# Scores of two heads together, biases read ready-made, a split last output column, and a planner with other durations

## The chip, the cores and the metric

The kernel runs as one launch on one core of a Trainium2 chip. The metric is device microseconds (us) of that core, all shapes and types as the reference gives them (float32 throughout). A core has a tensor engine (PE, with weight loads shown apart as PEld), a vector engine (DVE), a scalar engine (ACT), a GpSimd engine (POOL), a sync engine (SP) that here issues all large DMAs, an SBUF, and a PSUM of eight banks of 128 x 512 float32 into which PE writes.

## The reference, cut to what matters

Two transformer blocks over 256 tokens and a model width of 2048, batch 1, one layer each.

```
# block 1: native sparse attention + conformer conv, then a conv-GLU FFN (5632 wide)
h = rms_norm(x); proj = h @ w_in                       # q, kv of 3 branches, gates, conv input
for each of 16 heads (4 kv heads): three softmaxes
    compressed: 15 block keys   s = q.k_cmp + bias[bucket(t - (16 n + 31))], masked
    selected, window: 256 keys  s = q.k     + bias[bucket(t - s)], masked (causal)
    out = gate_0 * p_cmp v_cmp + gate_1 * p_sel v_slc + gate_2 * p_win v_win
u = a * sigmoid(gate); depthwise conv of 31 taps; layer_norm; silu
x += concat(attention, conv) @ w_out
x += conv_glu_ffn(rms_norm(x));  x = rms_norm(x)
# block 2: MLA + gated linear attention, then a gated FFN, both modulated by ada = silu(c) @ w_ada
x += gate_m * rms_norm(mix(h) @ w_out)
f  = (silu(h @ w_gate) * (h @ w_up)) @ w_down          # 5632 wide
x += gate_f * rms_norm(f)
```

With 256 tokens there are four selection blocks and all of them are chosen, so the selected and the window branch are plain causal attention over 256 keys of 64 channels.

## The kernel before

**Weights and the main stream.** All weight matrices lie in DRAM in the order in which they are used, cut into chunks of 128 x 1024 (`MCS`). `load_raw` brings chunks from SP's queue. For precision each chunk is split in two float32r parts, `wh` on ACT (`split_h`) and `wl` on DVE (`split_l`), three chunks ahead (`LA`); `wh` has four buffers and `wl` three. Activations lie split in the same way (high and low part). A product is then three float32r matmuls: high x high, high x low, low x high (`run_group`). A chunk of two K tiles and four output tiles takes 24 matmuls of 256 columns. Groups (`GROUPS`) run in a fixed order: w_in (conv input c0, c1, kvc, c2, kk, gt, q0, q1, c3, vv, q2, q3), w_out in three parts (oa: heads' outputs 0 to 3, ob: 4 to 7, oz: the conv's channels), FFN 1, block 2 and last `g2_0` to `g2_3`, the down projection: its weights (512 columns) move, the tokens are stationary, and the two halves of 128 tokens (u = 0, 1) have a bank each. A group owns two or four of the eight PSUM banks until its evacuation.

**The planner.** While the program is written out, Python keeps an estimated clock per engine (`Clock.note`: cost by columns). All work that is not the main stream is a generator ("side"). `tick`, called every two K tiles, issues a step of a side if its inputs are ready by the estimated PE clock; a low-priority side (the conv) only runs while the estimated DVE clock is at most `LAG` = 1 us ahead of PE's. `need(n)` holds a step until n banks are free and, unless over 3 us of the group are left, enough stay over for the next group. `later` postpones an evacuation until PE's estimated end. The engines run what they were given in that order; a wrong estimate shows as a wait on the chip. Nearly every instruction is issued by one helper, line 306, so the rows say L306 and the tile names tell them apart.

**Side work of block 1.** `conv_gen`: 31 taps on 8 channel tiles on DVE (tile `cacc`), then the layer norm, whose result `ch`, `cl` is the input of the oz groups. `bias_gen`: a one-hot table (`oht`) times the 32 x 16 bias table on PE, once for distances (then stored to DRAM as `dtab` and read back per head pair, skewed, as tile `B`) and in 15 matmuls of 16 columns for the compressed keys (`cbias`). `att_gen`, per head: scores against `kz` (keys of one kv head in 64 of 128 rows, the other 64 rows zero, so that a 128-row q tile of two heads can be used) and `kcz`, 512 + 256 + 2 x 16 columns in float32, which PE does in two passes each; on DVE bias, mask and maximum (one custom instruction per branch, an add and a maximum for the compressed keys); exp and scaling on ACT; eight transposes on PE; copies `PT` on ACT; then per pair the products with V. `att_driver` starts a head when the one before has its scores and when the head `PB` = 3 before it is transposed.

**The end.** `finish` follows the last matmul: for each token half sum of squares, root, reciprocal, four multiply-adds of 512 columns on DVE and their four stores.

Of the kernel before, what the change touches and what calls it, by code (L numbers as in the profile page):

```python
# [143 lines left out]
PB = 3  # L144
# [4 lines left out]
AHEAD = 2  # L149
SKIP = 48  # L150
# [43 lines left out]
OH = Layout([("ohr", 384), ("ohf", 512)])  # L194
CA = Layout([("mix_g", 16), ("ffn_g", 16), ("relb", 16), ("cmask", 32), ("conv_w", 248), ("conv_b", 8), ("ln_g", 8),
# [3 lines left out]
OFF_C = 271  # L199
# [14 lines left out]
def _onehot(dist, width):  # L214
    o = np.zeros((128, width), np.float32)
    i = np.arange(len(dist))
    o[_bucket(dist), i] = 1.0
    o[32, i] = dist < 0
    return o


def pack_small(inp):
# [21 lines left out]
    for tt in range(2):  # L244
        cm[:, tt, :15] = (16 * np.arange(15)[None] + 31) <= (tt * 128 + t)[:, None]
    relb = np.zeros((33, 16), np.float32)
    relb[:32] = f["rel_bias"][:, HORD]
    relb[32] = NEG
    pos = f["cmp_pos"][0]
    oh = put(OH, dict(ohr=_onehot(np.arange(384) - 127, 384), ohf=_onehot(np.arange(512) - OFF_C, 512)))  # L250
    ca = put(CA, dict(
        mix_g=cols(f["mix_norm_g"][0]), ffn_g=cols(f["ffn_norm_g"][0]), relb=relb,
        cmask=cm.reshape(128, 32), conv_w=f["conv_w"][0].reshape(31, 8, 128).transpose(2, 1, 0).reshape(128, 248),
# [27 lines left out]
    return dict(vec=vec, fv=fv, oh=oh, ca=ca, cb=cb, w1=c(w1), wada=c(wada), x=c(x), pos=c(f["positions_2"]))  # L281
# [12 lines left out]

class Engine:
# [5 lines left out]
    def __getattr__(self, op):  # L301
        f = getattr(self.eng, op)

        def issue(*x, **k):
            self.clock.note(self.name, op, x)
            return f(*x, **k)  # L306
        return issue


class Clock:  # L310
# [4 lines left out]
    def __init__(self):  # L315
        self.t = dict(PE=0.0, DVE=0.0, ACT=0.0)
        self.dep, self.ends, self.n, self.last = 0.0, {}, 0, None

    def note(self, eng, op, x):
# [18 lines left out]
        start = max([self.t[eng], self.dep] + [v + self.LAT for k, v in self.ends.items() if k != eng])  # L338
# [35 lines left out]
class Kern:  # L374
    def __init__(self, nc, tc, a, dump=None, stop=None):
# [11 lines left out]
        self.hl = {}  # L387
# [140 lines left out]
    def later(self, f, norm):  # L528

        self.pending.append((self.clock.t["PE"] + Clock.LAT, f, norm))  # L530
# [21 lines left out]
    def run_group(self, g):  # L552
# [5 lines left out]
        src = self.src  # L558
# [10 lines left out]
        kl = len(g["ks"]) - 1  # L569
# [3 lines left out]
        for mi in g["mcs"]:  # L573
# [6 lines left out]
            h, l = self.next_mc(mi)  # L580
            t["PE"] = max(t["PE"], self.l_end.pop(mi))
            for u in range(nt if g["mode"] == "w" else 2):
                o = ps[u][:min(n, 128)] if g["mode"] == "w" else ps[u][:, :n]
                for q, k in enumerate(m["ks"]):
                    xh, xl = src(k, N)
                    if g["mode"] == "w":
                        c = slice(q * n + u * 128, q * n + u * 128 + min(n, 128))
                        p = ((h[:, c], xh), (h[:, c], xl), (l[:, c], xh))
                    else:
                        c, ts = slice(q * n, q * n + n), slice(u * 128, u * 128 + 128)  # L590
                        p = ((xh[:, ts], h[:, c]), (xl[:, ts], h[:, c]), (xh[:, ts], l[:, c]))
                    for i, (a, b) in enumerate(p):
                        self.mm(o[:, :b.shape[1]], a, b, k == 0 and i == 0, k == kl and i == 2)
                    if q % GRAN == GRAN - 1 and (u, k) != (nb - 1, m["ks"][-1]):
                        self.tick()
            self.emitted += 1
            if mi != g["mcs"][-1]:
                self.tick()
        ev = self.evac[key]
# [5 lines left out]
        self.tick()  # L605

# [127 lines left out]
    def build(self):  # L734
        nc, tc = self.nc, self.tc
        with ExitStack() as es:
# [10 lines left out]
            with ExitStack() as ph:  # L747
# [12 lines left out]
                if not self.stop:  # L760
                    self.finish()
# [26 lines left out]
    def block1_setup(self):  # L788
# [12 lines left out]
        self.kz = P.tile([128, 4, 2, T], F32, name="kz")  # L801
        self.V = P.tile([128, 2, 2, 4, 64], F32, name="V")
        self.Gt = P.tile([128, 2, 8, 2, 3], F32, name="Gt")
        self.cbias = P.tile([128, 2, 8, 2, 16], F32, name="cbias")
        self.kcz = P.tile([128, 4, 16], F32, name="kcz")
# [6 lines left out]
        g.memset(self.kz, 0.0)  # L812
        g.memset(self.kcz, 0.0)
        g.memset(self.vz, 0.0)
        g.memset(self.cbias, NEG)
# [26 lines left out]
        self.side(self.bias_gen())  # L842
# [105 lines left out]
    def bias_gen(self):  # L948
        while "ss" not in self.flags:
            yield  # L950
        oh = self.early.tile([128, OH.n], F32, name="oht", tag="g2")
        self.sy.dma_start(oh, self.a["oh"])
        ohr, ohf = (oh[:33, o:o + n] for o, n in OH.at.values())
        yield 8.0
        yield from self.need(1)
        o = self.bank()
        self.mm(o[:16, :384], self.ca("relb", 0, 16)[:33], ohr)
        yield
        tr = self.early.tile([16, 384], F32, name="tabr", tag="tok")
        self.act(tr, o[:16, :384], AF.Copy)  # L960
        self.free(o)
        self.dtab = self.dp.tile([16, 384], F32, name="dtab")
        self.sy.dma_start(self.dtab, tr)
        yield
        yield from self.need(1)
        bk = self.bank()
        o = bk[:, :256].rearrange("p (n h) -> p n h", n=16)
        for w in range(15):
            c = OFF_C - 31 + 128 - 16 * w
            self.mm(o[:, w], ohf[:, c:c + 128], self.ca("relb", 0, 16)[:33])  # L970
        yield

        for tt, w, n in ((0, 8, 7), (1, 0, 15)):
            self.v.tensor_copy(self.cbias[:, tt].rearrange("p a u n -> p (a u) n")[:, :, :n],
                               o[:, w:w + n].rearrange("p n h -> p h n"))
        self.free(bk)

# [8 lines left out]
    def cmp_gen(self):  # L986
        yield
        for kv in range(2):
# [23 lines left out]
            if kv == 0:  # L1012
# [3 lines left out]
                dst = self.kcz.rearrange("p (b u) n -> p u b n", u=2)  # L1016
                for u in range(2):
                    pr = slice(64 * u, 64 * u + 64)
                    self.v.tensor_copy(dst[pr, u, :, 0:15], src[pr, u])
# [75 lines left out]
    def att_driver(self):  # L1095
# [10 lines left out]
        for n in range(16):  # L1106
            while f"q{n // 2}" not in self.flags or n >= PB and f"T{n - PB}" not in self.flags or \
                    n and f"S{n - 1}" not in self.flags:
                yield
            self.side(self.att_gen(n))  # L1110
            yield ATT
# [5 lines left out]
    def load_B(self, p):  # L1117
        B = self.att.tile([128, 2, T], F32, name="B", bufs=2)
        d = self.dtab
# [4 lines left out]
    def att_gen(self, n):  # L1124
# [3 lines left out]
        h = 2 * (p // 4) + u  # L1128
        q = self.qT[p]
        yield  # L1130
        yield from self.need(2)
        S1, S0 = self.bank(), self.bank()
        self.mm(S1, q[:, 128:], self.kz[:, h].rearrange("p r s -> p (r s)"))
        self.mm(S0[:, 0:256].rearrange("p (r s) -> p r s", r=2), q[:, :128], self.kz[:, h, :, :128])
        for tt in range(2):
            self.mm(S0[:, 256 + 16 * tt:272 + 16 * tt], q[:, tt * 128:tt * 128 + 128], self.kcz[:, h])
        self.flags.add(f"S{n}")
        yield
# [6 lines left out]
        rs = A.tile([128, 2, 3], F32, name="rs", bufs=6)  # L1145
        for r in range(2):
# [6 lines left out]
        self.free(S1, S0)  # L1153
        if u == 0 and p < 7:
# [6 lines left out]
        for tt in range(2):  # L1161
            self.act(sc[:, tt], sc[:, tt], AF.Exp, bias=mx[:, tt, 0:1], accum_out=sm[:, tt, 0:1])
# [6 lines left out]
        for tt in range(2):  # L1169
            self.stt(Pc[:, tt, 0:16], sc[:, tt], rs[:, tt, 0:1], self.ca("cmask", 16 * tt, 16), OP.mult, OP.mult)  # L1170
# [780 lines left out]
    def tok_gen(self):  # L1951
# [6 lines left out]
        self.ssq = self.f2.tile([128, 2, 4], F32, name="ssq")  # L1958
# [41 lines left out]
    def finish(self):  # L2000
        R = self.rp.tile([128, T], F32, name="sd")[:, :2]
        x = self.XT.rearrange("p (c a) t -> p c (a t)", a=2)
        for tt in range(2):
            r, f = R[:, tt:tt + 1], self.f[:, tt, 1536:]
            self.square(f, tt, 3)
            self.v.tensor_reduce(r, self.ssq[:, tt], axis=AX, op=OP.add)
            self.act(r, r, AF.Sqrt, scale=1.0 / D, bias=self.eps)
            self.tt(f, f, self.gpb[1][:, 1], OP.mult)
            self.v.reciprocal(r, r)
            for j in range(4):  # L2010
# [25 lines left out]
```

## Time and profile before

| | |
|---|---|
| median of 3 runs | 2206.18 us (2204.81 to 2206.24) |
| profiled execution | 2205.54 us, span 2203.8 us from the first to the last instruction |
| PE, PEld | 98%, 94% of the span busy, 17465 matmuls |
| DVE | 77% |
| ACT | 53% (1179.5 us) |
| POOL | under 1% |
| DMA | 496.51 MB from SP's hardware queue, 63.6% of 16 engines' span |
| chain that ended last | PE 89%, DVE 6%, ACT 2%, issue 1%, DMA 1% |

The page's busy share of PE is an upper bound, since matmuls are pipelined and their ends modelled; starts are what is measured. In the tables of stretches a row is: stretch, length, then for PE, PEld, DVE, ACT and POOL the busy us and the number of instructions, then the granted share of PE's clock, the DMA engines' share and GB/s.

### The profile page before, as it was taken

The numbers are of one execution on the slowest core, as the hardware profiler recorded it, in microseconds if no ns is written. First come the engines' busy times: TensorE is split into PE (matmuls) and PEld (weight loads), VectorE is DVE, ScalarE is ACT, GpSimd is POOL, SyncE is SP. The second block draws the span as 40 slices with busy tenths as digits, with TensorE's granted clock in tenths as the row PEclk, the third lists the DMA queues.
The fourth block names the chain that finished last, engine by engine and source line by source line (L and its number), as shares of the span: only waits on it lengthen the run. The fifth ranks groups of instructions, "written<-read, shape, count | busy, mean of one in ns | idle before, by whom it ended". The sixth has DMA issues, their size and how long they took to land.

```text
span 2203.8 us, 42192 instructions
## 1 busy us (share of the span) xinstructions
PE 2167.6 (98%) x17465; PEld 2081.5 (94%) x17465; DVE 1692.8 (77%) x2611; ACT 1179.5 (54%) x1805; POOL 5.1 (0%) x18
## 2 busy tenths in 40 slices
PE   8999999999999999999999999999999999999997
PEld 7998889999999999999999889989998999899986
DVE  7998988999998699999988666678676665554455
ACT  5447686655553355555556664466444444444443
POOL 0000000000000000000000000000000000000000
PEclk9999999999999999999999999999999999999999
DMA  6554325788888788888855334646776775555553
GB/s 232 192 178 152 130 82 194 254 322 325 310 326 323 276 316 316 323 319 306 302 201 180 134 134 137 209 153 211 251 260 244 254 252 189 194 188 176 192 194 131
DMA packets 86784, 499.20 MB, mean 227 GB/s; under 512 B 9648, under 2 KB 12096, under 8 KB 40128
## 3 DMA queue, kind: packets, MB, share of 16 engines
q1 hardware_dynamic: 86592, 496.51, 63.6%
q8 instruction: 136, 2.23, 0.4%
q14 instruction: 56, 0.46, 0.1%
HBM read 494.35 MB, written 2.12 MB: 225 GB/s over the span
## 4 chain that ended last, share of the span: by engine, by line
PE 89%; DVE 6%; ACT 2%; issue 1%; DMA 1%; SPq 0%; DVEq 0%; ACTq 0%
PE ps L306 89%; DVE wl L306 2%; DMA raw<-in_wst_dram 1%; DVE cacc L306 1%; ACT wh L306 0%; DVE X L306 0%; DVE ac L306 0%; ACT L306 0%; DVE og L306 0%; ACT P L306 0%; DVE nt L306 0%; ACT X L306 0%; ACT ge L306 0%; DVE XT L306 0%; DVE ss L306 0%
## 5 line engine op out<-in xcount | busy, mean ns | idle before, releaser
L306 PE MATMUL ps<-X,wh 128*128 128x256 f32 (+1 forms) x7680 | 1330.3, 277 | 5.1 <-ACT X L306 2.9
L306 ACT ACTIVATE wh<-raw 128x1024 fp32r<-128x1024 f32 (+2 forms) x741 | 782.8, 1058 | 837.6 <-PE ps L306 781.2
L306 DVE TENSOR_TENSOR wl<-raw,wh 128x1024 fp32r<-128x1024 f32 (+2 forms) x741 | 898.9, 1215 | 393.8 <-PE ps L306 339.4
L306 PEld LDWEIGHTS ps<-X,wh 128*128 128x128 f32 x7680 | 1161.5, 188 | 11.4 <-ACT X L306 3.5
L306 PE MATMUL ps<-X,wl 128*128 128x256 f32 (+1 forms) x3840 | 1060.2, 276 | 4.8 <-DVE wl L306 4.8
L306 PEld LDWEIGHTS ps<-X,wl 128*128 128x128 f32 x3840 | 722.1, 188 | 6.0 <-DVE wl L306 6.0
L306 DVE SCALAR_TENSOR_TENSOR ac<-wa,cs,ac 128x512 f32<-128x512 f32 x360 | 269.5, 749 | 6.8
L306 PE MATMUL ps<-hid,wh 128*128 128x256 f32 x1408 | 239.5, 275 | 0.0
L306 PE MATMUL ps<-wh,hid 128*128 128x512 f32 x704 | 216.5, 388 | 0.0
L306 PEld LDWEIGHTS ps<-hid,wh 128*128 128x128 f32 x1408 | 212.0, 188 | 0.0
L306 PE MATMUL ps<-hid,wl 128*128 128x256 f32 x704 | 193.6, 275 | 0.0
L306 PEld LDWEIGHTS ps<-wh,hid 128*128 128x128 f32 x704 | 131.9, 188 | 27.4
L306 PE MATMUL ps<-wl,hid 128*128 128x512 f32 x352 | 136.6, 388 | 0.0
L306 PEld LDWEIGHTS ps<-hid,wl 128*128 128x128 f32 x704 | 132.2, 188 | 0.0
L306 DVE SCALAR_TENSOR_TENSOR cacc<-upad,cat,cacc 128x256 f32<-128x256 f32 x240 | 99.6, 476 | 0.3 <-ACT cacc L306 0.2
L306 PEld LDWEIGHTS ps<-wl,hid 128*128 128x128 f32 x352 | 66.1, 188 | 13.5
L306 DVE SCALAR_TENSOR_TENSOR y<-vt,fv,y 128x256 f32<-128x256 f32 x176 | 73.3, 478 | 0.0
L306 PE MATMUL ps<-wh,X 128*128 128x512 f32 x192 | 60.7, 397 | 0.0
L306 ACT ACTIVATE y<-ps,fv 128x256 f32<-128x256 f32 x84 | 49.3, 587 | 0.0
L306 PE MATMUL ps<-o,wh 128*128 128x256 f32 x256 | 46.8, 283 | 1.2 <-ACT o L306 1.1
L306 ACT ACT_TABLE_LOAD x30 | 38.5, 1283 | 9.9 <-DMA XT<-in_x_dram 4.9
L306 PEld LDWEIGHTS ps<-wh,X 128*128 128x128 f32 x192 | 35.3, 188 | 6.6
(321 smaller groups left out, 1726.7 us busy)
## 6 DMA issues: line engine op xcount, KB each, us to landing
raw<-in_wst_dram SPq DMA_DIRECT2D x363, 1024.0 KB, 4.9
wa<-in_wada_dram SPq DMA_DIRECT2D x192, 512.0 KB, 6.9
raw<-in_wst_dram SPq DMA_DIRECT2D x4, 768.0 KB, 4.5
raw<-in_wst_dram SPq DMA_DIRECT2D x4, 512.0 KB, 5.4
B<-dtab SPq DMA_DIRECT2D x8, 256.0 KB, 5.2
out_dram<-og SPq DMA_DIRECT2D x8, 256.0 KB, 2.7
XT<-in_x_dram SPq DMA_DIRECT2D x3, 512.0 KB, 6.8
w<-in_w_dram SPq DMA_DIRECT2D x2, 512.0 KB, 5.7
```

Source lines behind the costliest of these rows:

```text
L306: return f(*x, **k)
```

## The change

The scores of the two heads of a pair are issued by one generator (`score_gen`), head after head in turn; each uses only the 64 rows of its own q and keys (`kk`, without zero rows; `kc2` for the compressed keys), and four banks at a time. The biases come from DRAM as an input (`bias_rows`); the compressed keys' biases are a strided view of the same tile `B`; `bias_gen` and its tiles go. `PB` is 4. For the last three chunks of the last group the matmuls of token half 0 are issued first, for all three chunks, then those of half 1; `last_add` and `last_scale` do what `finish` did, half by half. The planner's costs change for PE and ACT, and it adds `DRAIN` behind PE.

```diff
-PB = 3
+PB = 4
+TAIL = 3
+def bias_rows(rel_bias):
+    d = np.arange(384) - 127
+    return np.where(d < 0, np.float32(NEG), rel_bias[_bucket(d)].T).astype(np.float32)[HORD]
+DRAIN = 0.16
 # Clock.note
-            c = (n * 2 if op == "transpose" else n if x[1].dtype == F32R else max(n, m) * (4 if m > 64 else m / 32)) / 2400 + 0.002
+            if r:
+                c = n * 17 / 16 / 2400
+            elif op == "transpose":
+                c = n * 2 / 2400 + 0.002
+            else:
+                c = max(n, m) * (4 if m > 64 else m / 32) * (0.5 if x[1].shape[0] == 64 else 1) / 2400 + 0.002
+            if r != self.r:
+                c += 0.09
-            c = 0.06 + n * 0.9e-3
+            c = 0.05 + n * 0.83e-3 if psum else 0.185 + n * 0.77e-3
+            c += 0.093 if "accum_out" in k else 0
+            if f not in ANY and f != self.table:
+                self.table = f
+                c += 1.28
-        start = max([self.t[eng], self.dep] + [v + self.LAT for k, v in self.ends.items() if k != eng])
+        start = max([self.t[eng], self.dep] + [v + self.LAT + (DRAIN if e == "PE" else 0) for e, v in self.ends.items() if e != eng])
 # later
-        self.pending.append((self.clock.t["PE"] + Clock.LAT, f, norm))
+        self.pending.append((self.clock.t["PE"] + Clock.LAT + DRAIN, f, norm))
 # run_group
+            us = range(nb)
+            if n_mc >= ends:
+                held.append((m, hl))
+                us = (0,)
...
+        if held:
+            self.later(lambda: self.last_add(0, ps[0]), False)
+            for m, hl in held:
+                for q in range(len(m["ks"])):
+                    self.products(g, ps[1], 1, m, q, hl, N)
+                    self.tick()
+            self.later(lambda: self.last_add(1, ps[1]), False)
 # ev_kk
-                for u in range(2):
-                    pr = slice(64 * u, 64 * u + 64)
-                    self.tt(self.kz[pr, 2 * b + u, br], ps[2 * br + b][pr, :T], self.R[pr], OP.mult)
+                self.tt(self.kk[:, b, br], ps[2 * br + b][:, :T], self.R, OP.mult)
 # att_driver, per pair p
+            while f"q{p}" not in self.flags or 2 * p + 1 >= PB and f"T{2 * p + 1 - PB}" not in self.flags or \
+                    p and f"M{2 * p - 1}" not in self.flags:
                 yield
+            self.side(self.score_gen(p))
+            yield 2 * ATT
+    def score_gen(self, p):
+        q, b = self.qT[p], p // 4
+        yield
+        yield from self.need(4)
+        S = [(self.bank(), self.bank()) for _ in range(2)]
+        rows = [slice(64 * u, 64 * u + 64) for u in range(2)]
+        for u, r in enumerate(rows):
+            self.mm(S[u][0], q[r, 128:], self.kk[r, b].rearrange("p r s -> p (r s)"))
+        for u, r in enumerate(rows):
+            self.mm(S[u][1][:, 0:256].rearrange("p (r s) -> p r s", r=2), q[r, :128], self.kk[r, b, :, :128])
+        for tt in range(2):
+            for u, r in enumerate(rows):
+                self.mm(S[u][1][:, 256 + 16 * tt:271 + 16 * tt], q[r, tt * 128:tt * 128 + 128], self.kc2[r, b, 0:15])
+        for u in range(2):
+            self.side(self.att_gen(2 * p + u, *S[u]))
 # att_gen: head 1 of a pair waits for M of head 0
-        self.tt(sc, S0[:, 256:288].rearrange("p (t n) -> p t n", t=2), self.cbias[:, :, p, u], OP.add)
-        self.v.tensor_reduce(mx[:, :, 0], sc, axis=AX, op=OP.max)
+        for tt, c in enumerate(cmp):
+            bias = bass.AP(tensor=B.tensor, offset=B.offset + 96 + 128 * tt, ap=[list(B.ap[0]), [-16, c.shape[1]]])
+            self.add_max(c, S0[:, 256 + 16 * tt:256 + 16 * tt + c.shape[1]], bias, mx[:, tt, 0:1])
+    def last_add(self, tt, ps):
+        f = self.f[:, tt, 1536:]
+        q = self.f2.tile([128, 512], F32, name="q", tag="u")
+        for e in range(2):
+            c = slice(256 * e, 256 * e + 256)
+            self.tt(f[:, c], ps[:, c], f[:, c], OP.add)
+            self.act(q[:, c], f[:, c], AF.Square, accum_out=self.ssq[:, tt, 3 + e:4 + e])
+        self.last_f = self.f2.tile([128, 512], F32, name="lf", bufs=2), *getattr(self, "last_f", ())
+        self.tt(self.last_f[0], f, self.gpb[1][:, 1], OP.mult)
+        if tt:
+            self.last_scale(0, (2, 3), self.last_f[1])
...      # reduce, root, reciprocal as in finish
+        self.last_scale(tt, range(4) if tt else (0, 1), self.last_f[0])
```

`last_scale(tt, js, last)` does the multiply-add of 512 columns and the store for each j in js.

## Rows read from the trace of the kernel before

**Rows 1.** The page, busy us, share of the span and instructions:

```profile
PE 2167.6 (98%) x17465; PEld 2081.5 (94%) x17465; DVE 1692.8 (77%) x2611; ACT 1179.5 (54%) x1805; POOL 5.1 (0%) x18
```

**Rows 2.** Busy time by stretch, block 1's side work:

```profile
57.00:310.00 253.00, 249.91 (x2001) 230.43 (x2001) 234.12 (x609) 159.54 (x370) 0.57 (x2) 1.00 0.45 152
105.00:160.00 55.00, 54.51 (x490) 53.64 (x489) 52.20 (x101) 24.81 (x28) 0.57 (x2) 1.00 0.51 173
310.00:345.00 35.00, 32.44 (x272) 29.98 (x267) 25.50 (x38) 25.37 (x46) 0.00 (x0) 1.00 0.30 95
```

**Rows 3.** Busy time by stretch, behind the bias matmuls:

```profile
53.55:56.96 3.41, 3.41 (x19) 3.41 (x18) 1.44 (x4) 0.00 (x0) 0.00 (x0) 0.50 0.84 295
56.96:60.37 3.41, 3.41 (x32) 3.41 (x32) 3.34 (x6) 1.79 (x2) 0.00 (x0) 1.00 0.06 19
```

**Rows 4.** Groups by shape, 35 to 345 us, PE (busy, mean ns, idle before):

```profile
L306 PE MATMUL ps<-kz,qT 128*128 128x512 f32 x32 | 16.4, 596 | 0.4 <-DVE qT L306 0.4
```

**Rows 5.** Timeline of PE: bias matmuls, a head's scores, products with V:

```profile
46.35 0.28 PE L306 MATMUL ps<-X,wl 128*128 128x256 f32 x1
47.30 0.51 PE L306 MATMUL ps<-X,wh 128*128 128x256 f32 x2
48.71 0.28 PE L306 MATMUL ps<-X,wl 128*128 128x256 f32 x1
48.91 3.52 PE L306 MATMUL ps<-cat,oht 33*128 33x16 f32 x30
52.36 0.51 PE L306 MATMUL ps<-X,wh 128*128 128x256 f32 x2
...
161.65 0.28 PE L306 MATMUL ps<-X,wl 128*128 128x256 f32 x1
161.76 1.45 PE L306 MATMUL ps<-kz,qT 128*128 128x512 f32 x4
163.41 0.48 PE L306 MATMUL ps<-X,wh 128*128 128x256 f32 x2
...
226.72 0.39 PE L306 MATMUL ps<-X,wh 128*128 128x256 f32 x2
227.06 0.39 PE L306 MATMUL ps<-X,wh 128*128 128x256 f32 x2
227.49 0.65 PE L306 MATMUL ps<-PT,vz 128*64 128x256 f32 x4
227.97 1.47 PE L306 MATMUL ps<-PT,V 128*64 128x256 f32 x16
229.37 0.51 PE L306 MATMUL ps<-X,wh 128*128 128x256 f32 x2
```

**Rows 6.** Groups by shape, 35 to 345 us, DVE:

```profile
L306 DVE TENSOR_TENSOR kz<-ps,R 64x256 f32<-64x256 f32 x8 | 3.4, 421 | 0.1
```

**Rows 7.** Waits of DVE, 57 to 338 us (us in total, times, longest):

```profile
DVE rs L306 <- ACT sc L306: 9.1, 5, 2.9
```

**Rows 8.** Timeline: the last sum of the conv's taps; the first oz matmul:

```profile
312.73 0.69 DVE L306 TENSOR_TENSOR upad<-upad,cacc 128x512 f32<-128x512 f32 x1
...
345.88 0.28 PE L306 MATMUL ps<-ch,wh 128*128 128x256 f32 x1
```

**Rows 9.** Timeline of PE: scores of heads 6 and 15:

```profile
236.06 0.59 PE L306 MATMUL ps<-kz,qT 128*128 128x512 f32 x1
...
303.36 0.59 PE L306 MATMUL ps<-kz,qT 128*128 128x512 f32 x1
```

**Rows 10.** Timeline of DVE at the end:

```profile
2192.09 0.69 DVE L306 TENSOR_TENSOR og<-ps,og 128x512 f32<-128x512 f32 x1 [0.67 <-PE ps L306]
...
2193.55 2.74 DVE L306 SCALAR_TENSOR_TENSOR og<-og,sd,XT 128x512 f32<-128x512 f32 x4
2196.21 0.15 DVE L306 TENSOR_REDUCE sd<-ssq 128x1 f32<-128x4 f32 x1
...
2197.06 2.74 DVE L306 SCALAR_TENSOR_TENSOR og<-og,sd,XT 128x512 f32<-128x512 f32 x4
```

More of the change, by code (lines that the diff above doesn't have):

```diff
@@ L304, in issue @@
         def issue(*x, **k):
-            self.clock.note(self.name, op, x)
+            self.clock.note(self.name, op, x, k)
             return f(*x, **k)
@@ L316, in __init__, with note @@
         self.t = dict(PE=0.0, DVE=0.0, ACT=0.0)
-        self.dep, self.ends, self.n, self.last = 0.0, {}, 0, None
-    def note(self, eng, op, x):
+        self.dep, self.ends, self.n, self.last, self.table, self.r = 0.0, {}, 0, None, None, True
+    def note(self, eng, op, x, k):
         n = int(np.prod(x[0].shape[1:]))
@@ L322, in note @@
             m = x[0].shape[0]
[L323 to L325 removed]
+            r = op != "transpose" and x[1].dtype == F32R
+            if r:
[6 more added lines that the diff above has]
+                c += 0.09
+            self.r = r
+        elif eng == "ACT":
+            f = x[2]
+            psum = x[1].tensor.name[:2] == "ps"
+            c = 0.05 + n * 0.83e-3 if psum else 0.185 + n * 0.77e-3
[3 more added lines that the diff above has]
+                c += 1.28
         elif op == "reciprocal":
@@ L572, in run_group @@
         t = self.clock.t
-        for mi in g["mcs"]:
+        ends = len(g["mcs"]) - (TAIL if g is GROUPS[-1] else 0)
+        held = []
+        for n_mc, mi in enumerate(g["mcs"]):
             m = MCS[mi]
@@ L579, in run_group @@
                 self.idle()
-            h, l = self.next_mc(mi)
+            hl = self.next_mc(mi)
             t["PE"] = max(t["PE"], self.l_end.pop(mi))
[L582 to L595, printed above, removed]
+            us = range(nb)
+            if n_mc >= ends:
+                held.append((m, hl))
+                us = (0,)
+            for u, q in [(u, q) for u in us for q in range(len(m["ks"]))]:
+                self.products(g, ps[u], u, m, q, hl, N)
+                if q % GRAN == GRAN - 1 and (u, m["ks"][q]) != (nb - 1, m["ks"][-1]):
+                    self.tick()
             self.emitted += 1
@@ L605, in run_group, with products @@
         self.tick()
+    def products(self, g, bank, u, m, q, hl, N):
+        n, (h, l), k = g["n"], hl, m["ks"][q]
+        xh, xl = self.src(k, N)
+        if g["mode"] == "w":
+            o = bank[:min(n, 128)]
+            c = slice(q * n + u * 128, q * n + u * 128 + min(n, 128))
+            p = ((h[:, c], xh), (h[:, c], xl), (l[:, c], xh))
+        else:
+            o = bank[:, :n]
+            c, ts = slice(q * n, q * n + n), slice(u * 128, u * 128 + 128)
+            p = ((xh[:, ts], h[:, c]), (xl[:, ts], h[:, c]), (xh[:, ts], l[:, c]))
+        for i, (a, b) in enumerate(p):
+            self.mm(o[:, :b.shape[1]], a, b, k == 0 and i == 0, k == len(g["ks"]) - 1 and i == 2)
     def xsrc(self, k, N=T):
@@ L946, in conv_gen @@
             self.flags.add(f"conv{b}")
[L948 to L976, printed above, removed]
     def ev_kvc(self, ps):
@@ L1105, in att_driver @@
         self.done, self.PT = 0, {}
-        for n in range(16):
-            while f"q{n // 2}" not in self.flags or n >= PB and f"T{n - PB}" not in self.flags or \
-                    n and f"S{n - 1}" not in self.flags:
+        for p in range(8):
+            while f"q{p}" not in self.flags or 2 * p + 1 >= PB and f"T{2 * p + 1 - PB}" not in self.flags or \
+                    p and f"M{2 * p - 1}" not in self.flags:
                 yield
-            self.side(self.att_gen(n))
-            yield ATT
+            self.side(self.score_gen(p))
+            yield 2 * ATT
         while self.done < 16:
@@ L1122, in load_B, with att_gen @@
         self.Bt[p] = B
-    def att_gen(self, n):
+    def score_gen(self, p):
[13 more added lines that the diff above has]
+            self.side(self.att_gen(2 * p + u, *S[u]))
+        yield
+    def att_gen(self, n, S1, S0):
         A = self.att
         p, u = divmod(n, 2)
[L1128 to L1138, printed above, removed]
+        while u and f"M{n - 1}" not in self.flags:
+            yield
         B = self.Bt[p][:, u]
@@ L1145, in att_gen @@
         rs = A.tile([128, 2, 3], F32, name="rs", bufs=6)
+        cmp = [sc[:, tt, :(7, 15)[tt]] for tt in range(2)]
         for r in range(2):
@@ new lines, in last_scale @@
+    def last_scale(self, tt, js, last):
+        x = self.XT.rearrange("p (c a) t -> p c (a t)", a=2)
+        for j in js:
+            o = self.f[:, tt, 512 * j:512 * j + 512]
+            f = last if j == 3 else o
+            self.stt(o.rearrange("p (c n) -> p c n", c=2), f.rearrange("p (c n) -> p c n", c=2), self.rt[tt],
+                     x[:, 2 * j:2 * j + 2, 256 * tt:256 * tt + 256], OP.mult, OP.add)
+            self.sy.dma_start(self.a["out"][128 * tt:128 * tt + 128, 512 * j:512 * j + 512], o)
```

70 lines of the change are left out of this document (22 added, 48 removed).

## The prediction

> **What bounds the kernel now.** I read the page first: PE is busy 98% of the span, and the chain of waits is PE's for nine tenths of it [rows 1]. So I ask of each edit what it takes out of PE's stream, and then whether another engine lets PE have it. The second view is the table of stretches. In 57 to 310 us, where conv and attention of block 1 are side work, PE idles 3.1 of 253 us, but DVE is busy 234.1 of them, 92.5%; in 105 to 160 us it reaches 94.9%, the most of the stretches shown [rows 2]. PE is the bound there with DVE close behind. The third view is PE's timeline around the instructions that go. Behind the stretches, the last tap sum of the conv ends at 313.4 and oz, which needs the layer norm that follows it, begins at 345.9 [rows 8]: a chain of DVE, ACT and PE work lies between, beside the oa and ob groups. At the end only DVE works for 7.7 us [rows 10].
>
> The sum is made against the profiled execution, 2205.54 us, whose span is 2203.8; the median of the runs, 2206.18, is 0.64 above it.
>
> **Scores of two heads.** Three main-stream matmuls of 256 columns take 0.34 us (226.72 to 227.06), 0.113 each [rows 5]. A head's scores begin at 161.76 and the stream goes on at 163.41, that is 1.65 us; the two matmuls after it take 0.48 where such a pair takes 0.39, so the way back costs 0.09 more. Together 1.74 a head, 3.48 a pair. The 32 passes of 512 columns [rows 4] are 16 heads times two passes. After the change a pass has 64 rows, and the two heads lie in different halves of the rows. Whether they run beside each other, the trace of before does not show for rows. The nearest rows are the products with V, whose two heads lie in different halves of the output columns: four passes of 256 columns take 0.48 (227.49 to 227.97), and the sixteen passes behind them 1.40. One after the other the four would take 0.87, by 256 columns at the rate of the scores, since 1.65 us pay for two passes of 512, two of 256 and four short ones, or about 0.43 and 0.22. So column halves overlap fully, two for one. Bounds for the row halves: no overlap, 3.48 us a pair as now, a saving of nothing; full overlap, one head's 1.65, plus 0.09 to get in (after 227.06 three matmuls end at 227.40, and the V products begin at 227.49) and 0.09 to get out, plus some 0.04 for the second head's offset: 1.87. I take full overlap, the row of the nearest kind: 1.61 saved on each of eight pairs, **12.9 us**.
>
> The rule that speaks against it is in the Trainium skill, "TensorE: Matmul & The Clock Gate", Part 3, "The mechanism": matmuls start and end strictly in program order. If a head's two passes were issued back to back, only the second pass of one head would lie beside the first of the next, three steps for two, and by this rule the pair would take up to 0.8 us more and the change save 6.5 us of scores instead of 12.9. The V rows disagree, as far as column halves go.
>
> **Biases.** The one-hot matmul takes 47.30 less 46.35 less one matmul, 0.84 us, and the thirty passes of 16 columns 52.36 less 48.71 less 0.11, 3.54 [rows 5]. Both stand in a dense stream: **4.4 us** go. Behind them the granted clock is 0.50, that is 1.2 GHz, from 53.55 to 56.96, and 19 matmuls fit where the next stretch of the same length, at 2.4 GHz, has 32 [rows 3]. What PE did before it fell were those thirty passes of 16 columns. With them gone the stream there is as dense as behind it, and I take the fall to go too: 13 matmuls, **1.5 us**. Bounds: nothing, if it falls all the same, and 1.5. The loads and stores that go lie on SP's queue among weight loads that have three chunks of lead, and the reads of B no longer wait for a store; I count nothing. The memsets of the zero rows go from POOL, which is busy 5.1 us in all [rows 1]: nothing. The fourth buffer per head (`PB`) lets a pair start while the pair before it is still held; its price is in the slower rival.
>
> **The end.** From the last half's add (2192.09) to the end of its last multiply-add (2199.80) DVE needs 7.71 us, and half 0's reduction, root and four multiply-adds lie inside [rows 10]. In the new order half 0 has 18 matmuls of 512 columns of time, 4.1 us at twice 0.113 each, which is enough for its add, root and two multiply-adds. Left behind PE are two adds of 256 (0.72 for both), one product (0.6), two multiply-adds of half 0 (half of 2.74), then from the reduction to the multiply-adds 0.85 as from 2196.21 to 2197.06, then 2.74: 6.3 us. **1.4 us** go, between 0 (if half 0 is not done in time) and 3.5 (all of half 0 out of it). The stores behind the last one stay.
>
> **DVE's and ACT's share.** `ev_kk` has four instructions instead of eight of 0.42 us [rows 6], 1.7 us less. The compressed scores have two instructions per head for two; between none and one more of 0.42 each for 16 heads, I take none. So DVE needs some 232.4 us in a stretch that PE, 12.9 us quicker, would pass in 240.1: 96.8%. At the 94.9% of its best stretch it needs 244.9. The conv is of low priority, so what DVE can't fit moves back, the taps end later against PE, and oz waits: I put **4.8 us** back. Bounds: nothing, and all 12.9, if DVE stays at 92.5%.
>
> **The planner's durations.** It counted 256/2400 + 0.002 = 0.109 us for a main matmul that takes 0.113, and for ACT's short exps far less than they take: DVE waited 9.1 us, five times, for ACT's compressed exps [rows 7]. With truer costs DVE's gaps shrink, which is why I trust the 94.9%. What it can give PE itself is at most PE's idle time, 3.1 us to 310 and 2.6 to 345 [rows 2], 5.7 with no gain elsewhere; below nothing, new orders can cost as much. I take half of it, **3 us**. Main-stream work outside is the same.
>
> **Sum.** 12.9 + 4.4 + 1.5 + 1.4 = 20.2 out, 4.8 back, 3 out: 2205.5 - 18.4 = **2187 us**.
>
> **The rivals.**
> - Row halves don't overlap. For: no row of before shows it. Against: column halves do. Nothing of the 12.9 and nothing to give back: 2205.5 - 7.3 - 3 = 2195. By the ordering rule above, half of it: 2205.5 - 13.8 - 3 = 2189.
> - DVE becomes the bound fully. For: 92.5% already, and a layer-norm chain of 32 us behind the taps [rows 8], beside PE work that does not grow. Against: its waits for ACT should shrink. Then PE waits ahead of oz for what the scores saved: 2205.5 - 7.3 = 2198.
> - All of it comes through, as DVE fills up and the planner removes what idles: 2205.5 - 20.2 - 5.7 = 2180.
> - Slower: a pair now waits for four free banks at once. In the oa and ob groups, one chunk long, the reserve for the next group is always asked, so five of the six banks that the group leaves must be free, and the previous group's two, transposes and V products use the same six. Heads 6 to 15 now start from 236.06 to 303.36 [rows 9], nine steps of 7.5, 15 us a pair; ob needs the last of them. If a pair takes 19 us, four steps make the last one 16 us late: all that the scores saved turns into waits, and 16 less 7.3 is lost, 2214. It decides from 1.8 us more per pair on. Against it: four banks are given back by DVE within two heads' maxima, a few us in 15.
> - No change: new waits of block 2's side work take what block 1 gains.
>
> **How the numbers follow.** Forecast (2182 to 2192) 0.47, the ordering rule's half 0.05, no overlap 0.12, DVE the bound 0.14, all of it 0.12, slower 0.06, no change 0.04. The range reaches from 2178, a little under the full gain, to 2200, over DVE as the bound with a planner that gains nothing. What a measurement can tell from no change is about 0.2%, 4.4 us. Every case but the last two is below 2201.8: faster 0.90, same 0.04, slower 0.06.
>
> **What would show it.** In the timeline a pair's passes start two by two, and the stream resumes 1.8 to 1.9 us after it left; if 3.4, the rows don't overlap. No half clock near 54 us. The first oz matmul near 329 instead of 345.9 with the forecast, near 340 if DVE is the bound, and then DVE's stretch over 97% busy or PE waiting there for `ch`. From the last add to the last multiply-add 6.3 us. It would be wrong altogether if pairs in oa stand more than 17 us apart, or if PE's idle time grows in block 2, which no edit touches but the planner's costs.

## The result, and the profile after

The changed kernel takes 2194.37 us (2194.27 to 2196.29) where the kernel before, run beside it, takes 2206.21: ratio 0.9947, 95% interval 0.9931 to 0.9962. It is faster by 11.8 us. That is inside the range given (2178 to 2200), and 7 us short of the 2187 forecast. The profiled execution takes 2194.42, its span 2192.6 of before's 2203.8. The page, for [rows 1]:

```profile
PE 2155.6 (98%) x17433; PEld 2072.5 (95%) x17433; DVE 1687.5 (77%) x2639; ACT 1178.8 (54%) x1806; POOL 2.8 (0%) x15
```

**Where the 11.2 us of span come from.** Both kernels have the same 16344 main-stream matmuls (those that read `wh` or `wl`) in the same order. I call *lead* how much earlier one of them starts than in the trace of before. At the 49th oz matmul, from where the stream is dense, the lead is 4.9 us (346.45 for 351.35); it stays there through FFN 1, grows by 4.5 in block 2 (9.4 at the last matmul, 2182.22 for 2191.66), and 1.7 come from the tail behind it. On the way the lead had been 7.5 us at 51 us, 26.9 at 276 and 29.3 at 285.5, the last main-stream matmul ahead of the last pair's scores: over 24 us of it were lost again before the 49th oz matmul. Busy time by stretch up to that 49th oz matmul, first before, then after, then after's stretches at half clock, then, behind the dots, the stretch of [rows 2] and three inside it:

```profile
0.00:351.35 351.35, 338.08 (x2667) 312.59 (x2668) 305.38 (x725) 220.43 (x466) 3.81 (x13) 0.99 0.48 163
```

```profile
0.00:346.45 346.45, 327.13 (x2635) 303.69 (x2636) 300.89 (x751) 217.53 (x463) 1.50 (x10) 0.97 0.48 165
14.10:17.50 3.40, 3.04 (x14) 3.04 (x15) 3.40 (x8) 3.09 (x6) 0.00 (x0) 0.50 0.63 194
290.57:300.81 10.24, 8.02 (x34) 5.37 (x35) 9.96 (x50) 8.89 (x32) 0.00 (x0) 0.50 0.00 0
304.23:311.05 6.82, 6.01 (x29) 3.82 (x30) 5.96 (x16) 3.05 (x8) 0.00 (x0) 0.50 0.00 0
338.36:341.77 3.41, 3.30 (x16) 3.01 (x15) 1.12 (x1) 3.38 (x6) 0.00 (x0) 0.50 0.14 60
...
57.00:310.00 253.00, 243.98 (x2007) 224.43 (x2007) 232.04 (x649) 160.32 (x384) 0.56 (x2) 0.97 0.45 154
150.00:240.00 90.00, 90.00 (x697) 81.14 (x696) 80.80 (x250) 68.48 (x176) 0.00 (x0) 1.00 0.48 165
240.00:273.00 33.00, 33.00 (x291) 30.59 (x291) 28.89 (x106) 28.59 (x86) 0.00 (x0) 1.00 0.43 144
273.00:290.00 17.00, 15.56 (x138) 13.22 (x134) 16.47 (x59) 9.66 (x28) 0.00 (x0) 1.00 0.41 141
```

Before spent 6.8 us of PE time at 0.50, from 36.48 and from 53.55 [rows 3], which costs about half of it, 3.4; after 20.4, which costs 10.2. Counted at full clock, PE's work fell from 334.7 to 316.9 us, by 17.7. The rows give 11.5 for the scores (worked out below) and 4.4 for the biases; the other 1.8 is not accounted for, in a busy time whose ends are modelled. Against it stand 6.0 us more of idle PE (19.3 for 13.3) and 6.8 more lost to the clock; 17.7 - 12.8 = 4.9. PE was full from 150 to 273 us; then it ran out of other work, because ob needs the last pairs. DVE is busy 91.7% of 57 to 310 us, a little less than before. PE's timeline there, with the idle time ahead and what ended it, the first pair's scores above it and the first oz matmuls below:

```profile
155.87 0.28 PE L304 MATMUL ps<-X,wl 128*128 128x256 f32 x1
156.07 1.56 PE L304 MATMUL ps<-kk,qT 64*128 64x512 f32 x8
157.47 0.52 PE L304 MATMUL ps<-kc,qT 64*128 64x15 f32 x8
157.91 0.51 PE L304 MATMUL ps<-X,wh 128*128 128x256 f32 x2
158.25 0.28 PE L304 MATMUL ps<-X,wl 128*128 128x256 f32 x1
...
286.23 1.77 PE L304 MATMUL ps<-kk,qT 64*128 64x512 f32 x7
287.62 0.40 PE L304 MATMUL ps<-kc,qT 64*128 64x15 f32 x3
287.83 0.38 PE L304 MATMUL ps<-kk,qT 64*128 64x256 f32 x1
...
290.62 0.69 PE L304 MATMUL ps<-vecs,Pc 128*128 128x128 f32 x2 [2.06 <-DVE Pc L304]
292.21 1.54 PE L304 MATMUL ps<-vecs,P 128*128 128x128 f32 x6 [0.90 <-ACT P L304]
...
298.01 0.69 PE L304 MATMUL ps<-PT,vz 128*64 128x256 f32 x1 [1.19 <-ACT PT L304]
...
304.70 0.69 PE L304 MATMUL ps<-vecs,Pc 128*128 128x128 f32 x2 [2.36 <-DVE Pc L304]
...
308.11 2.77 PE L304 MATMUL ps<-PT,V 128*64 128x256 f32 x16
310.81 1.23 PE L304 MATMUL ps<-upad,vecs 128*128 128x256 f32 x4
...
311.70 0.47 PE L304 MATMUL ps<-o,wh 128*128 128x256 f32 x1
...
335.44 0.39 PE L304 MATMUL ps<-ch,wh 128*128 128x256 f32 x1 [0.71 <-ACT ch L304]
337.27 0.38 PE L304 MATMUL ps<-cl,wh 128*128 128x256 f32 x1 [1.44 <-DVE cl L304]
...
342.41 0.38 PE L304 MATMUL ps<-ch,wh 128*128 128x256 f32 x1 [0.75 <-ACT ch L304]
343.67 0.39 PE L304 MATMUL ps<-cl,wh 128*128 128x256 f32 x1 [0.88 <-DVE cl L304]
```

The stream resumes 1.84 us after the pair's first pass (the forecast's sign), and single records show the two heads' passes starting two by two, 6 to 7 ns apart, in seven of the eight pairs. In the last pair (286.23) the second head starts 0.43 us behind the first, one pass late. From 290 us PE waits for `Pc` and `P`, small steps of the last two pairs, and runs what it has at 1.2 GHz. Then two chains gate oz: the last pair's products with V (308.11) and the 27 us from them through ob, and the conv's `cl`, whose second half is done at 343.6. The chains touch: the first sums of the conv's layer norm on PE (`upad,vecs`, 310.81) stand in PE's order right behind the last pair's V.

The tail on DVE, for [rows 10]:

```profile
2182.64 0.76 DVE L304 TENSOR_TENSOR og<-ps,og 128x256 f32<-128x256 f32 x2 [0.48 <-PE ps L304]
...
2185.37 0.15 DVE L304 TENSOR_REDUCE sd<-ssq 128x1 f32<-128x5 f32 x1
...
2188.07 0.75 DVE L304 SCALAR_TENSOR_TENSOR og<-lf,r,XT 128x512 f32<-128x512 f32 x1
```

From the last half's add to the end of its last multiply-add, 6.18 us for 7.71.

### The profile page after: what moved, and what is told of

The parts are those of the page before. It is cut to its first block, busy times and chain, and to the rows that moved or that the text cites. A ratio compares the mean times of both kernels' runs of the same rounds, so it can differ in the third digit from the quotient of the medians.

```text
span 2192.6 us, 42160 instructions
## 1 busy us (share of the span) xinstructions
PE 2155.6 (98%) x17433; PEld 2072.5 (95%) x17433; DVE 1687.5 (77%) x2639; ACT 1178.8 (54%) x1806; POOL 2.8 (0%) x15
## 5 line engine op out<-in xcount | busy, mean ns | idle before, releaser
L304 DVE TENSOR_TENSOR wl<-raw,wh 128x1024 fp32r<-128x1024 f32 (+2 forms) x741 | 897.8, 1216 | 398.2 <-PE ps L304 344.0
L304 PE MATMUL ps<-hid,wh 128*128 128x256 f32 x1408 | 240.1, 275 | 0.0
L304 PEld LDWEIGHTS ps<-o,wh 128*128 128x128 f32 x256 | 38.8, 188 | 0.1
```

## The experiments

The rival explanations of the lost lead: *amount* (DVE has too much work before oz, as the prediction said), *banks* (a pair waits for four free ones), and *order* or *placement* (where the planner put the last pairs' steps and the conv's on the in-order engines). The columns, in us of each trace: start of the last pair's scores (of the last head's, where heads go alone), of its sixteen passes with V, of the first oz matmul, end of the second `cl`, start of the 49th oz matmul, its lead; the ratio of times is to before on the same chip.

| | last scores | V | oz | cl | 49th oz | lead | ratio |
|---|---|---|---|---|---|---|---|
| before | 303.4 | 317.7 | 345.9 | 348.6 | 351.4 | 0 | 1 |
| after | 286.2 | 308.1 | 335.4 | 343.6 | 346.4 | 4.9 | 0.9947 |
| e1 serial | 295.7 | 317.4 | 344.2 | 352.4 | 356.6 | -5.3 | 1.0001 |
| e2 taps | 302.7 | 322.3 | 346.0 | 282.2 | 351.4 | -0.1 | 0.9983 |
| e3 old costs | 291.3 | 311.3 | 338.9 | 338.9 | 344.3 | 7.0 | 0.9968 |
| e4 two banks | 293.8 | 320.1 | 347.8 | 336.2 | 353.2 | -1.9 | 0.9986 |
| e5 biases alone | 304.4 | 322.5 | 348.3 | 344.6 | 353.8 | -2.4 | 1.0012 |
| e6 costs alone | 305.4 | 329.7 | 357.1 | 338.1 | 362.6 | -11.2 | 1.0028 |
| e7 hold | 287.3 | 306.0 | 335.9 | 343.5 | 346.3 | 5.0 | 0.9962 |
| e8 place | 284.3 | 306.9 | 334.2 | 339.0 | 343.4 | 8.0 | 0.9944 |
| e9 fixed, taps | 285.4 | 305.4 | 333.0 | 341.1 | 344.0 | 7.4 | 0.9937 |
| e10 fixed, ACT | 286.5 | 307.3 | 334.5 | 342.7 | 346.8 | 4.5 | 0.9953 |
| e11 POOL | 311.7 | 339.2 | 364.1 | 366.0 | 369.5 | -18.1 | 1.0052 |
| e12 place 2 | 284.9 | 309.6 | 334.2 | 339.0 | 341.8 | 9.6 | 0.9936 |

**e1: heads one after the other**, four banks and all else as after.

```diff
         for u, r in enumerate(rows):
             self.mm(S[u][0], ...)
-        for u, r in enumerate(rows):
             self.mm(S[u][1][:, 0:256]...)
-        for tt in range(2):
-            for u, r in enumerate(rows):
+            for tt in range(2):
                 self.mm(S[u][1][:, 256 + 16 * tt:271 + 16 * tt], ...)
```

> The changed kernel, but each pair's scores are issued one head after the other (all of head 0, then all of head 1), so that the two halves of the rows can't run beside each other; all else is issued in the same order. A pair's scores should take about 3.4 us of PE's stream for 1.75. Order theory (PE waits at the end of oa because the last two pairs were issued late): the eight pairs cost 8 x 1.6, 13 us, and as the wait behind the last pair starts from its scores, most of it shows: slower than the changed kernel by 8 to 13 us, 2202 to 2207. Amount theory (DVE's amount of work is the bound of that stage): PE's lead there is idle time anyway, slower by 0 to 5 us, under 2200.

2205.06 us, 1.0001 (0.9992 to 1.0011): the whole gain is gone, as the order theory expected. A pair's scores take 3.23 us from first pass to the stream's return, 1.39 more than after, 11.1 for eight pairs; here PE's timeline:

```profile
155.83 1.55 PE L304 MATMUL ps<-kk,qT 64*128 64x512 f32 x4
157.22 0.17 PE L304 MATMUL ps<-kc,qT 64*128 64x15 f32 x1
157.23 0.69 PE L304 MATMUL ps<-kk,qT 64*128 64x512 f32 x1
157.25 0.48 PE L304 MATMUL ps<-kc,qT 64*128 64x15 f32 x3
157.76 1.02 PE L304 MATMUL ps<-kk,qT 64*128 64x512 f32 x3
158.62 0.51 PE L304 MATMUL ps<-kc,qT 64*128 64x15 f32 x4
159.06 0.38 PE L304 MATMUL ps<-X,wh 128*128 128x256 f32 x1
```

So the long passes of the two heads overlap only when they are issued in turn, and the change needs that for what it gains. At the border of the heads there is a little overlap: head 1's first pass starts at 157.23, ahead of three of head 0's four short ones.

**e2: half of the conv left out** (`for k in range(16)` instead of 31), planned anew.

> The changed kernel with 16 of the conv's 31 taps (taps 16 to 30 are left out), which takes some 48 us of low-priority work off DVE. Amount theory: PE's waits between 273 and 345 us (16 us in the changed kernel) nearly vanish, 2180 to 2185. Order theory: the waits for the conv's result ahead of oz go (5 us), but the last pairs still start at the end of oa and PE waits there as before or longer: 2188 to 2198.

2200.68, 0.9983 (0.9974 to 0.9993), slower than after: both missed. The taps end at 221 instead of 310 us, but the new plan scores pair 6 at 298.6 and not 281.4, and ob waits for its heads. DVE has 48 us less to do up to 345 us (253.0 for 300.9), and the stage is longer: amount alone is not the bound. `cl` is done 61 us sooner than in after, and the last pair's V comes 14 later.

**e3: after with the old durations** (`Clock.note`, `later` and `DRAIN` as before).

> The changed kernel planned with the durations of the kernel before (Clock.note as it was, no DRAIN). Order theory: another order in oa; if the last pairs' scores come earlier against the main stream, the stage is up to 10 us shorter, and the 2 to 4 us that block 2 gained are lost again: 2186 to 2194. Amount theory: the stage stays and block 2's gain goes: 2196 to 2200.

2197.70, 0.9968 (0.9955 to 0.9981). In block 1 the old durations place better (lead 7.0), but behind it nothing is won: 6.3 at the last matmul, where after goes from 4.9 to 9.4. The time lies in the amount theory's range, but the stage did not stay as it was.

**e4: two banks, then two more.**

```diff
-        yield from self.need(4)
-        S = [(self.bank(), self.bank()) for _ in range(2)]
+        yield from self.need(2)
+        S = [[self.bank()] for _ in range(2)]
...      # S1 of both heads
+        yield
+        yield from self.need(2)
+        for s in S:
+            s.append(self.bank())
```

> The changed kernel, but a pair takes its four banks in two steps: two for the 512-column scores of both heads, then two for the rest. Bank theory (a pair waits long for four free banks at one time): pair 6 starts earlier and PE's wait at the end of oa shrinks: 2184 to 2190. If the banks are only held up because DVE and ACT are behind: within 3 us of the changed kernel, or slower, since a pair then holds its first two banks longer.

2201.84, 0.9986 (0.9976 to 0.9995): slower than after, so the wait for four banks at once is not what holds the pairs up. The pairs' first pieces start sooner, their second later (293.8 for the last).

**e5 and e6: parts of the change alone on the kernel before.** e5 has only the biases from DRAM, e6 only the new durations.

> The kernel before with the laid-out biases alone (bias table from the host, shorter compressed-key rows; heads still one at a time, old planner durations, old last stage). The sum of the prediction: 4.4 us of bias matmuls and 1.5 us of half clock near 54 us go, so 2199-2201 us, with the lead of the main stream at 5-7 us by 60 us and kept. Placement theory: the lead of 5-7 us stands at 60 us, but what the stage up to 345 us keeps of it is decided by where the pieces of attention fall, so anything from 2199 to 2207 us; a lead at the first gated-output matmul (oz) below 3 us would show this.

> The kernel before with the planner's new durations alone: the same instructions in another order. The sum of the prediction: -3 us, 2203 us. From the run with the changed kernel planned by the old durations (2 us better up to 345 us, 4.4 us worse after it): 2 us lost up to the first oz matmul, about 4 us won after it, so 2202-2206 us. If the durations' effect up to 345 us goes with the scores' form (single heads or pairs) and not with the durations, the lead at oz is between -8 and +8 us, but the 4 us after it stay.

e5: 2207.10, 1.0012 (1.0003 to 1.0021). The lead rises from 0.3 at 46 us to 6.5 at 52, by 6.3 where the sum had 5.9. It is 6.5 again at 238, with some dips and one rise between, and -2.4 at oz, as the placement theory allowed: all of it was lost, and 2.4 more. e6: 2211.20, 1.0028 (1.0017 to 1.0039): the same instructions in another order lose 11.2 us up to the 49th oz matmul and 1.4 more in FFN 1, at a half clock from 445.4, then win 4.2 in block 2, much as after does (e5, with old durations, wins nothing there). Time and lead lie beyond all that was expected of e6.

**e7 and e8: after, placed otherwise.**

```diff
 # e7
-HOLD = 3.0
+HOLD = 1.0
 # e8
+    conv(3)
     q(0)
     q(1)
-    conv(3)
...
-ATT = 4.5
-HOLD = 3.0
+ATT = 3
+HOLD = 2
...
-LAG = 1.0
+LAG = 1.5
```

> The changed kernel with one constant of the planner changed: side work may take free banks until 1 us (not 3 us) before the end of a group of the main stream, so the step that needs four free banks at once starts sooner. Placement theory (the last two pairs start late because they wait for four banks while the next group's are reserved): pair 6 starts near 273 us and not 281, pair 7 near 285, TensorE's waits for Pc and P at 290-311 us shrink from 6.5 us to under 4 us, 2189-2193 us. Amount theory (VectorE's work up to the first oz matmul sets it): the pairs start earlier, but the oz matmuls wait for cl as before, 2193-2196 us.

> The changed kernel with the same work placed otherwise: the last convolution group c3 goes ahead of the first group of queries, and three constants of the planner differ (wait between scorings 3 and not 4.5 us, banks reserved 2 and not 3 us ahead, convolution taps let in up to 1.5 and not 1.0 us of backlog on VectorE). Placement theory: the last pairs start near 273 and 285 us, the lead of the main stream at oz is 9-11 us and not 4.9 us, and 2187-2191 us. Amount theory: same work on VectorE, so the lead at oz stays at 4-6 us, 2193-2196 us.

e7: 2196.22, 0.9962 (0.9947 to 0.9977). Pair 6 starts at 275.0, near the time expected, pair 7 at 287.3, 2 later than expected, and V comes 2 us sooner; but `cl` is done when it was: nothing won, as the amount theory expected. e8: 2192.63, 0.9944 (0.9930 to 0.9959); V 1.2 us sooner, `cl` 4.6, lead 8.0, between the two theories' leads, and in time not told apart from after. So in after it is `cl` that holds the 49th oz matmul up: V alone sooner (e7) wins nothing, `cl` sooner does. V comes next: the table puts it 5.5 us behind, and to win more both must shorten.

**e9 and e10: the order kept, an engine relieved.** Here the planner still counts what is left out, so every instruction keeps its place; e9 leaves out every second tap, e10 narrows 64 normalisations on ACT to 16 columns.

```diff
 # e9
+                    elif k % 2:
+                        self.clock.note("DVE", "scalar_tensor_tensor", (y[:, e], x, w, y[:, e]), {})
 # e10
+    def narrow(self, x, f, **k):
+        self.clock.note("ACT", "activation", (x, x, f), k)
+        self.s.eng.activation(x[:, :16], x[:, :16], f, **k)
...
-                self.act(x, x, AF.Copy, scale=f)
+                self.narrow(x, AF.Copy, scale=f)
```

> The changed kernel with every instruction in the place it has there, but every second convolution tap left out (120 of 240, some 55 us of VectorE's 300 us up to 345 us; the convolution comes out other). Amount theory (VectorE's work sets the first oz matmul): the lead of the main stream at oz rises from 4.9 to 13-18 us, 2181-2186 us. Order theory (the last pairs of heads stand too late in the queues, and their steps wait for each other): the value product of the last pair stays within 3 us of 308 us, only the wait for cl ahead of the oz matmuls goes, lead 6-9 us, 2190-2193 us.

> The changed kernel with every instruction in its place, but the 64 normalisations of the probabilities on ScalarE made 16 columns wide in place of 128 and 256 (some 17 us less on ScalarE; the probabilities stay unnormalised). If ScalarE's durations are on the chain of the last pairs: two heads' share of it is 1.1 us a pair in the chain itself and some 5 us of queue, the last value product 3-6 us earlier than 308 us, lead at oz 7-11 us, 2188-2192 us. If VectorE's amount or the order alone sets it: 2193-2196 us.

e9: 2191.58, 0.9937 (0.9917 to 0.9957). Up to the 49th oz matmul DVE is busy 258.3 us:

```profile
0.00:343.95 343.95, 325.23 (x2634) 302.57 (x2635) 258.31 (x631) 217.58 (x463) 1.50 (x10) 0.97 0.48 166
```

42.6 us less than after's 300.9, and the 49th oz matmul is 2.5 sooner, V 2.7: the order theory's numbers. PE's waits stand where they stood, first below; then come DVE's last tap sum and what PE does around it:

```profile
288.86 0.47 PE L304 MATMUL ps<-vecs,Pc 128*128 128x128 f32 x2 [1.51 <-DVE Pc L304]
291.07 0.92 PE L304 MATMUL ps<-vecs,P 128*128 128x128 f32 x6 [1.74 <-ACT P L304]
...
301.98 0.69 PE L304 MATMUL ps<-vecs,Pc 128*128 128x128 f32 x2 [2.50 <-DVE Pc L304]
...
304.48 0.69 DVE L304 TENSOR_TENSOR upad<-upad,cacc 128x512 f32<-128x512 f32 x1
...
305.40 2.77 PE L304 MATMUL ps<-PT,V 128*64 128x256 f32 x16
308.10 1.48 PE L304 MATMUL ps<-upad,vecs 128*128 128x256 f32 x4
```

The last rows also say why `cl` gained no more: the taps' last sum is done at 305.17, but the layer norm's first matmuls stand in PE's order behind V and start at 308.10. So e9 speaks of this order: in it, less work on DVE gives almost nothing. In e3, e8 and e12 these matmuls stand ahead of V, and `cl` is done 4.6 to 4.8 us sooner than in after; that the place does it was not tried by itself.

e10: 2194.96, 0.9953 (0.9937 to 0.9969), lead 4.5: nothing. ACT is busy 208.7 us up to 345 us for after's 217.5, so 8.8 us were taken away, half of what was expected: a normalisation of 16 columns still takes 0.30 us, where 128 take 0.39 and 256 take 0.50. That much of ACT's work is not it either.

**e11: GpSimd takes every third `wl`** of 22 groups, c3 behind vv, planned anew.

```diff
+        e = self.g if MCS[i]["g"] in POOLG and i % 3 == 0 else self.v
-            self.tt(l[:, a:b], ...)
+            e.tensor_tensor(l[:, a:b], ...)
```

> The changed kernel with every third subtraction that makes a low half of the weights (wl) in 22 groups of block 1's attention stage on GpSimd in place of VectorE (some 26 us less on VectorE), planned again with a duration of 2.2 us for it, the group c3 behind vv, and two constants of the planner as in the kernel placed otherwise. Same results by the same arithmetic. Amount and order theory both: room on VectorE and the last pairs at 270 and 282 us: lead at oz 10-14 us, 2184-2190 us, if GpSimd takes under 3 us for one. If it takes over 4 us, or slows VectorE while it runs: TensorE waits for wl, 2196-2215 us.

2217.38, 1.0052 (1.0035 to 1.0068), 2 us over the slower range expected. One subtraction takes 2.88 us in the mean, and taps on DVE stand still beside it. First POOL's group of the list by line (busy us, mean ns, idle ahead of them), then the timeline: one on POOL, and the three taps on DVE around it, which take 3.44 us where four take 1.67 at 101.43:

```profile
L305 POOL TENSOR_TENSOR wl<-raw,wh 128x1024 fp32r<-128x1024 f32 x23 | 66.1, 2876 | 261.6 <-PE ps L305 180.7 <-ACT wh L305 64.7 <-ACT P L305 16.1
```

```profile
101.43 1.67 DVE L305 SCALAR_TENSOR_TENSOR cacc<-upad,cat,cacc 128x256 f32<-128x256 f32 x4
...
70.95 2.55 POOL L305 TENSOR_TENSOR wl<-raw,wh 128x1024 fp32r<-128x1024 f32 x1 [5.50 <-PE ps L305]
...
70.75 3.44 DVE L305 SCALAR_TENSOR_TENSOR cacc<-upad,cat,cacc 128x256 f32<-128x256 f32 x3
```

**e12: after, placed a third way** (gt ahead of kk; ATT 3, HOLD 1, LAG 1.25).

> The changed kernel placed another way: the gate group gt ahead of the keys kk, and three constants of the planner differ (wait between scorings 3 and not 4.5 us, banks reserved 1 and not 3 us ahead, convolution taps let in up to 1.25 and not 1.0 us of backlog on VectorE). Two-chain theory (the first oz matmul waits for the later of the last pair's value product plus some 27 us and of cl): last pairs near 273 and 284 us, the last value product near 306 us, cl near 340 us, lead at oz 7-10 us, 2188-2192 us. Noise of placement (any other order is as likely to lose as to win, by up to 10 us): 2194-2202 us.

2191.34, 0.9936 (0.9922 to 0.9949), span 2188.7, lead 9.6, `cl` at 339.0 as expected, V 3.6 later than expected (and 1.4 later than in after, so the 4.7 us of lead come from `cl`). What is left waits for `cl` alone:

```profile
334.06 0.28 PE L304 MATMUL ps<-o,wl 128*128 128x256 f32 x1
339.02 0.38 PE L304 MATMUL ps<-cl,wh 128*128 128x256 f32 x1 [1.63 <-DVE cl L304]
```

It beats before, and its span is 3.9 us under after's; the intervals of the two ratios overlap.

## Why the prediction came out as it did

- **PE bounds, DVE close behind: right to 273 us, wrong behind it.** From there the chains of the last pairs and of the conv do. That the time is inside the range is in part luck: the give back was 8 us larger than in the sum, and the range was wide enough.
- **Scores, 12.9: right in kind, 11.5 by rows.** 0.09 to get in, 1.84, 0.11 to get out (157.91 to 158.25 for two matmuls that take 0.23): 2.04 a pair instead of 1.87, 1.44 saved. e1 gives 11.1. My half-way case, three steps for two, is not what happened: the passes of the two heads alternate in seven pairs (0, 7, 533, 540 ns), and e1, which issues head after head, loses nearly all the overlap. The rule of the Trainium skill that I weighed ("TensorE: Matmul & The Clock Gate", Part 3, "The mechanism": matmuls start in program order) does not hold to the letter across row halves here: in all eight pairs of e1 head 1's first pass starts ahead of three short passes of head 0 that were issued before it (157.23 against 157.25 and later), and in after's last pair a `kc` pass starts at 287.62, ahead of a `kk` pass at 287.83 that was issued before it.
- **Biases, 4.4, and the clock, 1.5.** Together 6.3 for 5.9: after's lead rises from 1.2 at 45 us to 7.5 at 51. The earlier half clock, at 36.48 in before, is gone too, and a new one at 14.1 gave that back in part. That a saving in a dense stream is kept was not so: e5 keeps none of it.
- **Tail, 1.4: 1.5 on DVE, 1.7 from the last matmul's start to the end.**
- **The failed step: "So DVE needs some 232.4 us in a stretch that PE, 12.9 us quicker, would pass in 240.1: 96.8%", and from it 4.8 us back.** What came back is 12.8, half as idle PE and half as half clock, and not by DVE's amount of work in this order: e9 takes 42.6 us from DVE and gets 2.5. DVE's work itself was right (232.0 us busy), but its share of 57 to 310 us is 91.7%, not near 97. (The bound, too, was off: at 92.5% the same sum gives 11.1 back, not 12.9.) I sized the give back by a busy share, when the end of the stage is set by two chains in a fixed order: in the table the first oz matmul follows the last pair's V by 24 to 30 us in every kernel, and the 49th comes 5.5 us after it or 2.8 to 4.4 after `cl`, whichever is later. After's V is 9.6 us sooner than before's, for PE's 17.7; its `cl` only 5.0, and that is the lead. Which step of the last pair's chain sets its 22 us from scores to V stays open: e9 takes 2 us from it, e10 1.
- **The planner, 3: 4.5, but elsewhere.** I bounded it by PE's idle time to 345 us, "no gain elsewhere". All of it lies in block 2; PE's wait of 1.6 us for `ac` near 1118, which before and e3 have, is gone; that is 1.6 of the 4.5. DVE's wait for the compressed exps is gone too (0.2 us of 9.1 [rows 7]), with no gain in the stage to show for it. e6 shows what I gave no price: a new order of the same work moved block 1 by 11 us.
- **The rivals.** Full DVE bound (2198) is near in time, and PE did wait for `ch` and `cl` as it said, but it falls by e9 and by DVE's 91.7%. The slower one got its sign (pairs 5 and 6 stand 29 us apart, 252.1 to 281.4, over the 17 that I said would make the forecast wrong altogether), not its price: PE was 27 us ahead by then, so the last pair is still 17 us sooner than in [rows 9]. e4 and e7 say that banks alone don't set the end.
- **The signs.** No half clock near 54, 1.84 and 6.18 us came true; oz at 335.4 is neither 329 nor 340, with PE waiting for `ch` and `cl`.

Open: whether an order exists that keeps all 17.7. The best run here keeps 9.6, its rest ending in `cl`; shortening the layer norm's chain behind the taps (34 us from the last tap, 309.5, to `cl`), or moving its matmuls ahead of V and nothing else, wasn't tried.

## What to carry to other kernels

Where side work must end before a later group, add up the chain from its last input to that group first; busy shares did not show it here, and what the main stream saves turns into waits once it runs ahead of that chain. To price an edit in a program placed by a planner, keep the order and change only the work (e9, e10): planned anew, the order alone moved this stage by -11 to +5 us against its neighbours. And when TensorE goes idle between short steps, look at the granted clock: here it cost as much as the waits (6.8 us more for 6.0).

## What the runs showed of the hardware

- Two float32 products with 64 rows each, in different halves of the rows, run fully beside each other if issued in turn (64x512: passes 6 to 7 ns apart in seven of after's eight pairs; 1.84 us for two heads, 3.23 head by head). Between the halves the order of starts is not strictly that of issue (e1 at 157.23, after at 287.62).
- The clock fell in after at 290.57, behind a wait of 2.06 us among transposes and scores, and stayed at 1.2 GHz in two stretches of 10.2 and 6.8 us while PE ran little but the last pairs' steps; with dense `o` matmuls from 311.7 it was 2.4 GHz again.
- GpSimd and VectorE exclude each other on these subtractions and taps: beside eight of the 23 a tap takes 2.58 to 2.66 us (0.48 alone) and ends 0.3 behind GpSimd, and one subtraction takes 6.2 beside a run of taps; the maxima, which read scores from PSUM, go on (0.41 to 0.42), but the small step behind them, with one input from SBUF, is held up to 2.39 (0.17 in after). The Trainium skill, "SBUF — State Buffer", section "SBUF: two separate sides", says that the port which the two share is an exclusive lock for a VectorE instruction with two SBUF inputs beside a GpSimd one that reads SBUF; the trace agrees.
